# Small matmuls of four heads in one burst, RWKV's two heads in turn, and sixteen columns ahead of h

## The chip, the cores and the metric

The kernel runs on one core of a Trainium2 chip. The metric is device time in microseconds (us), lower is better. The profile names the engines PE (TensorE, matmuls), PEld (TensorE, weight loads), DVE (VectorE), ACT (ScalarE), POOL (GpSimd) and SP (SyncE, which here issues most DMAs).

## The reference

A trunk of two layers on one sequence of 1024 tokens with 1024 features, all in float32. Of each layer this matters here:

```python
h = _rmsnorm(x, norm1_g[l]) * (1.0 + sc1) + sh1
(rw_r, rw_k, rw_v, gl_q, gl_k, gl_v, gl_g,
 rt_q, rt_k, rt_v, rt_g) = jnp.split((h @ w_in[l]).astype(f32), splits, axis=-1)
...
y = jnp.concatenate([y_a, y_b, y_c], axis=-1).astype(x.dtype) @ w_out[l]
x = x + gt1 * y
h = _rmsnorm(x, norm2_g[l]) * (1.0 + sc2) + sh2
x = x + gt2 * ((jax.nn.silu(h @ ffn_w_gate[l]) * (h @ ffn_w_up[l])) @ ffn_w_down[l])
```

`y_a` is RWKV-7 time mixing with 8 heads of 64. `y_b` is gated linear attention (GLA) and `y_c` is retention, each with 4 heads, keys of 32 and values of 64, in chunks of 64 tokens: inside a chunk scores times values, and between chunks a carried state:

```python
att = jnp.sum(q_[:, :, :, None, :] * k_[:, :, None, :, :] * dec, axis=-1)
return jnp.einsum('bhnm,bhme->bhne', att, v_)
...
inter = jnp.einsum('nbhcd,nbhde->nbhce', qc * jnp.exp(bc), s_prev)
```

## The kernel before

**Layout and halves.** Activations lie transposed, features on the 128 partitions and tokens along the columns. The sequence is worked in two halves of 512 tokens, so x is 8 tiles of 128x512 for each half. The order is: projection of layer 0 half 0, then of half 1; output projection and FFN of half 0; output projection of half 1 and projection of layer 1 half 0; FFN of layer 0 half 1; and so on with layer 1, one half behind the other.

**Dense matmuls.** `dense` (L200 to L211) makes one 128x512 output tile. Weights and activations are split into a high and a low float32r part, so each of 8 k steps has three matmuls: high weight on high activation (L207), high weight on low activation (L208), low weight on high activation (L209). Two PSUM banks named `psd` take turns. The weight tile is cast on ACT (L186) and its low part is made on POOL (L187).

**h.** The normalised activations are 16 tiles `h` (8 k steps, high and low), made in `norm_h` (L290 to L319). Each is 514 columns wide: the 512 tokens start at the third column, and the second column holds the last token of the half before, so that the LoRA matmuls of RWKV can read h shifted by one token (`hact(h, 1)`, L327). The FFN's own intermediate, `gh` and `gl`, lies in tiles of 512 columns that are read from the first.

**Streams.** The small work of the heads is written as Python generators. A generator yields a cost; `pump` (called in `dense` after each k step with 0.65) gives each stream that much times its rate, and the stream goes on while it has credit. So instructions of the streams are placed between dense matmuls in program order, each behind the dense matmul it follows. The rates are 1.8 for the heads and mixers of layer 0 half 0, 1.5 for RWKV's preparations that run ahead of them, and 0.8 for the rest. Waiting is left to semaphores. All engines run their own instructions in order. The constants AT1 to AT5, GL1 to GL4 and PR1 to PR9 are the costs that are yielded; `drain` runs what is left.

**PSUM for the streams.** `pmx` (L592 to L595) hands out banks in the turn pm, yA, px, yB, pm, yu, where pm has two buffers: six banks. RWKV with two units at once (layer 0 half 0) takes px and yB in turn for the matmuls here.

**GLA and retention** (`Attn`, L628 to L712). `scores` (L653 to L662) loops over 4 heads; for each it takes a bank, makes 8 matmuls, one for each chunk (L660: 32 rows of keys, 64x64 out, into the upper or lower half of the partitions by the chunk's parity), hands the bank to a sink, and yields AT1. GLA (L717 to L757) calls it 7 times: once with plain q and k (the sink copies on ACT), and once at each of 6 levels of blocks with decayed q and k (the sink is a predicated copy on DVE, L745). Retention calls it once (L774). `finish` (L664 to L712) transposes the keys, makes the chunk states (L672 on PE, L683 on DVE), and then for each head makes 8 matmuls scores times values (L697, 64 rows) and 8 matmuls query times state (L699, 32 rows) into one bank, yields AT5, copies it out on ACT (L701), and after each two heads calls `norm_tok` (L606 to L625).

**RWKV** (`rwkv`, L783). Each half of a layer has 4 units. `prep` of a unit builds W and bk, then for two groups of 4 chunks and the two heads j (rows 0 to 63 and 64 to 127) makes 4 matmuls (L871, 64 rows, 128 columns of weights and 128 of output) into a bank, which DVE masks into GB and W (L875, L876); PR3 is yielded after each.

An fp32 matmul of the program shows in the profile as two MATMUL instructions.

Of the kernel before, what the change touches and what calls it, by code (L numbers as in the profile page):

```python
# [10 lines left out]
F32 = mybir.dt.float32  # L11
F32R = mybir.dt.float32r
# [29 lines left out]
XV = 2  # L42
PR1 = 4.0
PR2 = 3.0
PR3 = 0.8
PR4 = 0.5
PR5 = 1.0
PR6 = 3.2
# [3 lines left out]
CH1 = 1.0  # L52
CH2 = 1.0
CH3 = 1.5
AT1 = 0.8
AT2 = 1.0
AT3 = 0.7
AT4 = 0.25
AT5 = 1.0
GL1 = 1.0  # L60
GL2 = 2.0
GL3 = 1.5
GL4 = 1.0
# [2 lines left out]
WHB = 3  # L66
WLB = 3
XPB = 11
AHEAD = 60
RATEP = 1.5  # L70
RATEN = 1.0
# [23 lines left out]
def trunk_kernel(ctx, tc, xT, cT, ada_w, pv, wfm, wo, wg, wu, wd, l1w, l2a, l2g, l2c,  # L95
# [3 lines left out]
    V, A, G, T, SY = nc.vector, nc.scalar, nc.gpsimd, nc.tensor, nc.sync  # L99
# [31 lines left out]
    def f32(ap):  # L131
        return ap.bitcast(F32)
# [126 lines left out]
    def rstd_of(x, idle=None):  # L259


        acc = wp.tile([128, 512], F32, tag="nr", name="acc", bufs=1)
        if idle:
            ps = bank()
        for k in range(KT):
            if idle:
                sq = idle.tile([128, 512], F32, tag="sq", name="sq", bufs=5)
            else:
                sq = acc if k == 0 else wp.tile([128, 512], F32, tag="n", name="sq", bufs=2)
            A.activation(out=sq, in_=x[k], func=AF.Square)  # L270
            if idle:
                T.matmul(ps, om, sq, start=k == 0, stop=k == KT - 1)
                if k == 0:

                    A.activation(out=lnt, in_=sq[:, 0:1], func=AF.Ln, bias=eps)
            elif k:
                V.tensor_tensor(out=acc, in0=acc, in1=sq, op=ALU.add)  # L277
        yield 8.0
        if not idle:
            ps = bank()  # L280
            T.matmul(ps, om, acc, start=True, stop=True)
        A.activation(out=acc, in_=ps, func=AF.Ln, bias=eps)
        rstd_last[:] = [A.activation(out=acc, in_=acc, func=AF.Exp, scale=-0.5).ins]
        yield 1.0
        return acc

    rstd_last = []
    hlast = {}

    def norm_h(x, l, hf, which, h, pool=hp, r=None, mods=None, E=V, idle=None):  # L290

        if r is None:
            r = yield from rstd_of(x, idle)
        gs = par.tile([128, 8], F32, name="gs", tag=f"gs{which}")
        g = P(l, "n1g" if which == 0 else "n2g")
        if mods is None:
            V.scalar_tensor_tensor(out=gs, in0=mod[l][:, 3 * which + 1, :], scalar=1.0, in1=g, op0=ALU.add, op1=ALU.mult)
        if which == 0 and hf == 0:
            hlast[l] = par.tile([128, KT, 2], F32, name="hlast", tag="hlast")
        for k in range(KT):  # L300
            h.append([pool.tile([128, 514], F32R, tag="h", name="h", bufs=16) for _ in range(2)])
            sh = mod[l][:, 3 * which, k:k + 1]
            t = wp.tile([128, 512], F32, tag="n", name="nt", bufs=2)
            hi, lo = (h[k][j][:, 2:514] for j in range(2))
            if mods is not None:
                mods(k)
                V.scalar_tensor_tensor(out=gs[:, k:k + 1], in0=mod[l][:, 3 * which + 1, k:k + 1], scalar=1.0, in1=g[:, k:k + 1],
                                       op0=ALU.add, op1=ALU.mult)
            (V if k < XV else E).tensor_tensor(out=t, in0=x[k], in1=r, op=ALU.mult)
            A.activation(out=t, in_=t, func=AF.Identity, scale=gs[:, k:k + 1], bias=sh)  # L310
            split(t, hi, lo, E)
            if which == 0:
                for j in range(2):
                    if hf == 0:
                        G.memset(f32(h[k][j][:, 0:2]), 0.0)
                        G.tensor_copy(hlast[l][:, k, j:j + 1], f32(h[k][j][:, 513:514]))
                    else:
                        G.tensor_copy(h[k][j][:, 1:2], hlast[l][:, k, j:j + 1])
            yield 1.0  # L319

    def norm_now(*a, **kw):
# [3 lines left out]
        return h  # L325

    def hact(h, shift=0):  # L327
        return lambda k, part: h[k][part][:, 2 - shift:514 - shift]

    xs_d = [[dram.tile([128, 512], F32, name=f"xs{k}{j}") for j in range(2)] for k in range(KT)]  # L330
    y_d = [[None if k < 4 else dram.tile([128, 512], F32, name=f"y{k}{j}") for j in range(2)] for k in range(KT)]
# [255 lines left out]
    R2 = [slice(0, 64), slice(64, 128)]  # L587
# [4 lines left out]
    def pmx(of="all"):  # L592

        cyc[of] += 1
        return bank4(BANKS[of][cyc[of] % len(BANKS[of])])  # L595
# [32 lines left out]
    class Attn:  # L628
# [23 lines left out]

        def scores(self, kd, qd, sink):  # L653

            for h in range(4):
                r = slice(32 * h, 32 * h + 32)
                ps = pmx()
                for c in range(8):
                    cc = slice(c * 64, c * 64 + 64)
                    T.matmul(ps[R2[c % 2], (c // 2) * 64:(c // 2) * 64 + 64], kd[r, cc], qd[r, cc], start=True, stop=True)  # L660
                sink(h, ps[:, :256].rearrange("p (a n) -> p a n", a=4))
                yield AT1  # L662

        def finish(self, att, qd, kd, dec, centre, scale):  # L664
            pool, hf, key = self.pool, self.hf, "S" + self.g
# [19 lines left out]
                yield AT4  # L685
            if hf == 0:
                G.tensor_copy(carry[key], Sa[:, 8, :])
            Ys = []
            for hp_ in range(2):
                Y = self.t("gqe", 2).rearrange("p (a j e) -> p a j e", a=4, j=2)  # L690
                for j in range(2):
                    h = 2 * hp_ + j
                    r = slice(32 * h, 32 * h + 32)
                    o = pmx()
                    oc = [o[R2[c % 2], (c // 2) * 64:(c // 2) * 64 + 64] for c in range(8)]
                    for c in range(8):
                        T.matmul(oc[c], att[h][R2[c % 2], c // 2, :], self.v(h, c), start=c < 2, stop=False)  # L697
                    for c in range(8):
                        T.matmul(oc[c], qd[r, c * 64:c * 64 + 64], Sa[r, c, :], start=False, stop=c > 5)  # L699
                    yield AT5  # L700
                    A.copy(Y[:, :, j, :], o[:, :256].rearrange("p (a e) -> p a e", a=4))  # L701
                Ys.append(Y.rearrange("p a j e -> p (a j) e"))
                norm_tok(Ys[-1], pool, self.tmp, EPS, centre)
            yield FY
# [78 lines left out]
    def rwkv(l, hf, ip, pool, B=1):  # L783
# [33 lines left out]
        def prep(q, k1, r1, v1, wt, sa):  # L817
# [47 lines left out]

            GB = pool.tile([128, 8, 128], F32, tag="GB", name="GB", bufs=B)
            for a in (0, 4):
                for j, r in enumerate(R2):
                    o, ps = R2[1 - j], ppx()
                    for c in range(a, a + 4):  # L870
                        T.matmul(ps[:, (c - a) * 128:(c - a) * 128 + 128], bk[r, c].rearrange("p s t -> p (s t)"), W[r, c, j, :],  # L871
                                 start=True, stop=True)
                    p3 = ps.rearrange("p (a t) -> p a t", a=4)
                    mk = gmask.unsqueeze(1).to_broadcast([128, 4, 128])
                    V.tensor_tensor(out=GB[r, a:a + 4, :], in0=p3[r], in1=mk[r], op=ALU.mult)  # L875
                    V.tensor_tensor(out=W[o, a:a + 4, j, :], in0=p3[o], in1=mk[o], op=ALU.mult)  # L876
                    yield PR3
            gl = GB[:, :, 0:64]

            nd = dram.tile([32, 32, 32], F32, tag="nd", name="nd", bufs=3)  # L880
# [309 lines left out]
    with pool("x0") as x0:  # L1190
# [4 lines left out]
        h = []  # L1195
# [177 lines left out]
```

## Time and profile before

| | us |
|---|---|
| median of 3 runs | 3398.83 |
| lowest, highest | 3397.83, 3406.38 |
| the profiled execution | 3401.25 |
| its span, first to last instruction | 3399.5 |

The stages of the profiled execution, read from which lines evict the dense tiles: projection of layer 0 half 0 until about 345 us, of half 1 until 655, output projection and first FFN until 1390, projection of layer 1 half 0 until 1629, FFN until 2207, projection of layer 1 half 1 until 2445, output projections and FFN half 0 of layer 1 until 3030, and the last FFN half to the end. The heads of GLA and retention run beneath the projections, those of layer 0 half 1 beneath the output projection and the start of the first FFN. RWKV's units run beneath the FFNs, save those of layer 0 half 0, which run beneath the projection of half 1.

In the lines quoted below, a row of a stage view gives start and end, length, busy time of each engine with its count, the granted TensorE clock as a share of full speed, the DMA share and GB/s. A row of the timeline gives start, duration, engine, line, operation, output tile and inputs, shape and count, and in brackets the idle time before it with what ended it. Matmuls are pipelined: durations overlap, and the pace is read from start to start.

### The profile page before, as it was taken

What the parts mean: (1) busy time and instruction counts of PE and PEld (TensorE: products, weight loads), DVE (VectorE), ACT (ScalarE), POOL (GpSimd) and SP (SyncE); (2) the same over time, 40 slices, a digit from 0 to 9 for tenths busy, and PEclk for the clock granted to TensorE, in tenths of its full rate; (3) what the DMA queues carried; (4) which work ended last, traced back from release to release, by engine and by line L of the source; (5) the groups of instructions that cost most, each with busy time, mean ns of one, the idle gap of its engine ahead of it and who ended that gap; (6) DMA issues with size and microseconds to landing.
All of it is one profiled execution on the core that took longest, in us unless ns stands there. A gap on an engine that the chain in (4) does not pass through costs nothing. (4 is left out here: it accounts for less than half of the span.)

```text
span 3399.5 us, 47488 instructions
## 1 busy us (share of the span) xinstructions
PE 3049.9 (90%) x18162; PEld 2326.1 (68%) x18162; DVE 1994.5 (59%) x3747; ACT 1113.9 (33%) x1703; POOL 1234.7 (36%) x825
## 2 busy tenths in 40 slices
PE   6897888799888888999988999899997989999998
PEld 4664666476676676776766777677576767778886
DVE  6565777576776655536766663624666666452223
ACT  4324323243233223524322322542432322342222
POOL 6313333123334334532333434533232433444443
PEclk8988889799989898999988999999897989999999
DMA  6744535434544224434433322543533323332332
GB/s 230 239 157 142 169 110 156 153 103 128 147 129 113 88 84 133 156 90 146 129 98 86 87 70 87 161 130 112 155 83 88 105 80 94 120 109 87 105 92 82
DMA packets 266835, 411.01 MB, mean 121 GB/s; under 512 B 71152, under 2 KB 149424, under 8 KB 266608
## 3 DMA queue, kind: packets, MB, share of 16 engines
q1 hardware_dynamic: 211312, 393.28, 37.2%
q10 hardware_dynamic: 55296, 14.70, 2.1%
q8 instruction: 143, 2.34, 0.3%
q14 instruction: 84, 0.69, 0.1%
HBM read 343.92 MB, written 63.96 MB: 120 GB/s over the span
## 5 line engine op out<-in xcount | busy, mean ns | idle before, releaser
L187 POOL TENSOR_TENSOR wl<-wr,wh 128x1024 fp32r<-128x1024 f32 (+2 forms) x508 | 1028.6, 2027 | 1744.2 <-ACT wh L186 1653.2
L207 PE MATMUL psd<-h,wh 128*128 128x512 f32 (+1 forms) x2208 | 933.2, 423 | 112.7 <-DVE sg L1100 65.7
L208 PE MATMUL psd<-h,wh 128*128 128x512 f32 (+1 forms) x2208 | 908.1, 411 | 12.1 <-DVE h L195 12.0
L209 PE MATMUL psd<-h,wl 128*128 128x512 f32 (+1 forms) x2208 | 905.1, 410 | 0.0
L186 ACT CAST wh<-wr 128x1024 fp32r<-128x1024 f32 (+2 forms) x507 | 440.8, 871 | 1142.0 <-PE psd L208 582.2
L207 PEld LDWEIGHTS psd<-h,wh 128*128 128x128 f32 (+1 forms) x2208 | 432.1, 196 | 249.9 <-DVE sg L1100 74.3
L208 PEld LDWEIGHTS psd<-h,wh 128*128 128x128 f32 (+1 forms) x2208 | 434.7, 197 | 117.2 <-DVE h L195 15.8
L209 PEld LDWEIGHTS psd<-h,wl 128*128 128x128 f32 (+1 forms) x2208 | 433.7, 196 | 103.2 <-issue 2.4
L207 PE MATMUL psd<-gh,wh 128*128 128x512 f32 x960 | 401.0, 419 | 25.9 <-DVE x L1114 14.0
L208 PE MATMUL psd<-gl,wh 128*128 128x512 f32 x960 | 385.0, 401 | 6.1 <-DVE gl L195 6.1
L209 PE MATMUL psd<-gh,wl 128*128 128x512 f32 x960 | 384.0, 400 | 0.0
L207 PEld LDWEIGHTS psd<-gh,wh 128*128 128x128 f32 x960 | 184.7, 193 | 78.6 <-issue 24.1
L1114 DVE SCALAR_TENSOR_TENSOR x<-psd,mod,x 128x512 f32<-128x512 f32 x192 | 143.2, 748 | 130.0 <-PE psd L209 128.4
L208 PEld LDWEIGHTS psd<-gl,wh 128*128 128x128 f32 x960 | 185.6, 193 | 47.0 <-DVE gl L195 9.3
L209 PEld LDWEIGHTS psd<-gh,wl 128*128 128x128 f32 x960 | 185.4, 193 | 40.6 <-POOL wl L187 0.3
L914 DVE TENSOR_TENSOR tm<-X,nl 128x60 f32<-128x60 f32 (+24 forms) x496 | 189.0, 381 | 14.6 <-DMA nl<-nd 0.2
L242 DVE SCALAR_TENSOR_TENSOR aw<-aw,cb 128x1024 f32<-128x1024 f32 x96 | 128.4, 1341 | 100.0 <-DMA aw<-in_ada_w 75.8
L916 DVE TENSOR_TENSOR X<-X,tm 128x60 f32<-128x60 f32 (+24 forms) x496 | 165.1, 333 | 15.3
L1100 DVE SCALAR_TENSOR_TENSOR sg<-sg,psd 128x512 f32<-128x512 f32 x88 | 60.1, 683 | 194.1 <-ACT sg L1099 193.9
L1103 DVE SCALAR_TENSOR_TENSOR sg<-sg,psd 128x512 f32<-128x512 f32 x88 | 60.1, 683 | 141.0 <-PE psd L209 140.8
L195 DVE TENSOR_TENSOR gl<-sg,gh 128x512 fp32r<-128x512 f32 x88 | 96.3, 1094 | 37.0 <-ACT gh L194 36.9
L277 DVE TENSOR_TENSOR acc<-acc,sq 128x512 f32<-128x512 f32 x63 | 96.3, 1528 | 30.9 <-ACT sq L270 29.4
(459 smaller groups left out, 3526.6 us busy)
## 6 DMA issues: line engine op xcount, KB each, us to landing
aw<-in_ada_w SPq DMA_DIRECT2D x96, 512.0 KB, 3.9
wr<-in_wfm SPq DMA_DIRECT2D x96, 512.0 KB, 3.7
wr<-in_wg SPq DMA_DIRECT2D x88, 512.0 KB, 3.6
wr<-in_wu SPq DMA_DIRECT2D x88, 512.0 KB, 3.6
wr<-in_wd SPq DMA_DIRECT2D x128, 256.0 KB, 2.7
wr<-in_wo SPq DMA_DIRECT2D x32, 512.0 KB, 3.6
wr<-in_wd SPq DMA_DIRECT2D x64, 192.0 KB, 2.4
x<-in_xT SPq DMA_DIRECT2D x32, 256.0 KB, 4.5
```

Of the source, the lines that this page charges most:

```text
L186: (E.copy if E is A else E.tensor_copy)(wh[:, :n], wr[:, :n])
L187: WS.tensor_tensor(out=wl[:, :n], in0=wr[:, :n], in1=f32(wh[:, :n]), op=ALU.subtract)
L195: E.tensor_tensor(out=lo, in0=src, in1=f32(hi), op=ALU.subtract)
L207: T.matmul(ps[:M], sh, act(k, 0), start=(k == order[0]), stop=False)
L208: T.matmul(ps[:M], sh, act(k, 1), start=False, stop=False)
L209: mark[:] = [T.matmul(ps[:M], sl, act(k, 0), start=False, stop=(k == order[-1])).ins]
L242: V.scalar_tensor_tensor(out=w, in0=w, scalar=0.5, in1=cb, op0=ALU.mult, op1=ALU.mult, accum_out=mod[l][:, rnd, k:k + 1])
L277: V.tensor_tensor(out=acc, in0=acc, in1=sq, op=ALU.add)
L914: V.tensor_tensor(out=tm[:, :nr, :n], in0=X[:, :nr, s:s + 1].to_broadcast([128, nr, n]), in1=nl[:, s, s + 1:32].unsqueeze(1).to_broadcast( ...
L916: V.tensor_tensor(out=X[:, :nr, s + 1:32], in0=X[:, :nr, s + 1:32], in1=tm[:, :nr, :n], op=ALU.add)
L1100: V.scalar_tensor_tensor(out=sg, in0=sg, scalar=1.0, in1=pg, op0=ALU.add, op1=ALU.mult)
L1114: V.scalar_tensor_tensor(out=x[m], in0=ps, scalar=mod[l][:, 5, m:m + 1], in1=x[m], op0=ALU.mult, op1=ALU.add)
```

## The change

- The four heads' `scores` take four banks at once; the loop runs over chunks outside and heads inside; the four sinks follow, and AT1 is yielded once. In `finish` the output matmuls of all heads come first: scores times values by head, then query times state with chunks outside and heads inside; AT5 is yielded once; the copies and both `norm_tok` follow.
- In `prep` the two heads' matmuls take a bank each and alternate; the masking of both heads follows; PR3 is yielded once for the pair.
- Costs: PR3 0.8 to 1.6, AT1 0.8 to 1.2, AT5 1.0 to 1.5, GL1 1.0 to 3.0.
- Tiles of h get 16 columns ahead of the tokens instead of 2: 528 columns, data from the 17th, the last token of the half before in the 16th. The squares at the very start (L267) have 4 buffers instead of 5.

```diff
-PR3 = 0.8
+PR3 = 1.6
-AT1 = 0.8
+AT1 = 1.2
-AT5 = 1.0
-GL1 = 1.0
+AT5 = 1.5
+GL1 = 3.0
+HP = 16
...
-                sq = idle.tile([128, 512], F32, tag="sq", name="sq", bufs=5)
+                sq = idle.tile([128, 512], F32, tag="sq", name="sq", bufs=4)
...
-            h.append([pool.tile([128, 514], F32R, tag="h", name="h", bufs=16) for _ in range(2)])
+            h.append([pool.tile([128, HP + 512], F32R, tag="h", name="h", bufs=16) for _ in range(2)])
...
-            hi, lo = (h[k][j][:, 2:514] for j in range(2))
+            hi, lo = (h[k][j][:, HP:] for j in range(2))
...
-        return lambda k, part: h[k][part][:, 2 - shift:514 - shift]
+        return lambda k, part: h[k][part][:, HP - shift:HP + 512 - shift]
...
         def scores(self, kd, qd, sink):
+            ps = [pmx() for _ in range(4)]
+            for c in range(8):
+                cc = slice(c * 64, c * 64 + 64)
+                for h in range(4):
+                    r = slice(32 * h, 32 * h + 32)
+                    T.matmul(ps[h][R2[c % 2], (c // 2) * 64:(c // 2) * 64 + 64], kd[r, cc], qd[r, cc], start=True, stop=True)
             for h in range(4):
-                r = slice(32 * h, 32 * h + 32)
-                ps = pmx()
-                for c in range(8):
-                    cc = slice(c * 64, c * 64 + 64)
-                    T.matmul(ps[R2[c % 2], (c // 2) * 64:(c // 2) * 64 + 64], kd[r, cc], qd[r, cc], start=True, stop=True)
-                sink(h, ps[:, :256].rearrange("p (a n) -> p a n", a=4))
-                yield AT1
+                sink(h, ps[h][:, :256].rearrange("p (a n) -> p a n", a=4))
+            yield AT1
...
-            Ys = []
+            Ys, os_ = [], [pmx() for _ in range(4)]
+
+            def oc(h, c):
+                return os_[h][R2[c % 2], (c // 2) * 64:(c // 2) * 64 + 64]
+
+            for h in range(4):
+                for c in range(8):
+                    T.matmul(oc(h, c), att[h][R2[c % 2], c // 2, :], self.v(h, c), start=c < 2, stop=False)
+            for c in range(8):
+                for h in range(4):
+                    r = slice(32 * h, 32 * h + 32)
+                    T.matmul(oc(h, c), qd[r, c * 64:c * 64 + 64], Sa[r, c, :], start=False, stop=c > 5)
+            yield AT5
             for hp_ in range(2):
                 Y = self.t("gqe", 2).rearrange("p (a j e) -> p a j e", a=4, j=2)
                 for j in range(2):
-                    h = 2 * hp_ + j
-                    r = slice(32 * h, 32 * h + 32)
-                    o = pmx()
-                    oc = [o[R2[c % 2], (c // 2) * 64:(c // 2) * 64 + 64] for c in range(8)]
-                    for c in range(8):
-                        T.matmul(oc[c], att[h][R2[c % 2], c // 2, :], self.v(h, c), start=c < 2, stop=False)
-                    for c in range(8):
-                        T.matmul(oc[c], qd[r, c * 64:c * 64 + 64], Sa[r, c, :], start=False, stop=c > 5)
-                    yield AT5
-                    A.copy(Y[:, :, j, :], o[:, :256].rearrange("p (a e) -> p a e", a=4))
+                    A.copy(Y[:, :, j, :], os_[2 * hp_ + j][:, :256].rearrange("p (a e) -> p a e", a=4))
...
             for a in (0, 4):
+                pss_ = [ppx(), ppx()]
+                for c in range(a, a + 4):
+                    for j, r in enumerate(R2):
+                        T.matmul(pss_[j][:, (c - a) * 128:(c - a) * 128 + 128], bk[r, c].rearrange("p s t -> p (s t)"),
+                                 W[r, c, j, :], start=True, stop=True)
                 for j, r in enumerate(R2):
-                    o, ps = R2[1 - j], ppx()
-                    for c in range(a, a + 4):
-                        T.matmul(ps[:, (c - a) * 128:(c - a) * 128 + 128], bk[r, c].rearrange("p s t -> p (s t)"), W[r, c, j, :],
-                                 start=True, stop=True)
-                    p3 = ps.rearrange("p (a t) -> p a t", a=4)
+                    o, p3 = R2[1 - j], pss_[j].rearrange("p (a t) -> p a t", a=4)
...
-                    yield PR3
+                yield PR3
```

More of the change, by code (lines that the diff above doesn't have):

```diff
@@ L314, in norm_h @@
                     if hf == 0:
-                        G.memset(f32(h[k][j][:, 0:2]), 0.0)
-                        G.tensor_copy(hlast[l][:, k, j:j + 1], f32(h[k][j][:, 513:514]))
+                        G.memset(f32(h[k][j][:, HP - 2:HP]), 0.0)
+                        G.tensor_copy(hlast[l][:, k, j:j + 1], f32(h[k][j][:, HP + 511:HP + 512]))
                     else:
-                        G.tensor_copy(h[k][j][:, 1:2], hlast[l][:, k, j:j + 1])
+                        G.tensor_copy(h[k][j][:, HP - 1:HP], hlast[l][:, k, j:j + 1])
             yield 1.0
```

## The prediction

> **What bounds the kernel now.** I read the page first, then the busy time by stage, then TensorE's timeline around the edited lines.
>
> ```profile
> span 3399.5 us, 47488 instructions
> ```
> ```profile
> 0.00:830.00 830.00, 689.41 (x4813) 496.87 (x4814) 553.95 (x1130) 279.19 (x432) 265.94 (x202) 0.87 0.50 158
> 830.00:1390.00 560.00, 487.36 (x2708) 379.21 (x2707) 382.12 (x712) 176.01 (x276) 220.29 (x165) 0.91 0.40 120
> 1390.00:1629.00 239.00, 233.27 (x1673) 169.96 (x1672) 106.81 (x212) 92.94 (x142) 72.69 (x37) 0.95 0.42 136
> 1629.00:2207.00 578.00, 521.76 (x2882) 408.20 (x2881) 364.43 (x674) 184.73 (x290) 227.69 (x153) 0.92 0.34 98
> 2207.00:2445.00 238.00, 231.99 (x1668) 169.19 (x1667) 106.90 (x212) 90.14 (x131) 75.09 (x46) 0.95 0.44 136
> 2445.00:3030.00 585.00, 531.83 (x2898) 415.34 (x2897) 365.27 (x672) 188.83 (x292) 219.86 (x135) 0.92 0.33 94
> 3030.00:3399.50 369.50, 354.30 (x1531) 287.29 (x1529) 114.99 (x135) 102.07 (x144) 153.14 (x88) 0.99 0.32 96
> ```
> The columns after the length are busy time of PE, PEld, DVE, ACT and POOL, then the granted clock. PE is the busiest engine in every stage, but not equally. I group the stages by what runs behind the dense matmuls. **Q** (1390 to 1629, 2207 to 2445) is the projection of layer 1 with the GLA and retention heads behind it: PE is busy 465 of 477 us, 97.5%. **T** (from 3030) is the last FFN half alone, 96%. **F** is the three stretches of output projection and FFN with RWKV behind: 1541 of 1723 us, 89%. **I** is the first 830 us, 83%. So PE time that is removed should shorten Q and T almost one for one, F less, I least. My weights, chosen from those shares and from what fills the rest (waits for DVE), are 0.95, 1, 0.75 and 0.6.
>
> **Part A: h starts 64 bytes in, not 8.** At the end of the kernel both kinds of dense matmul run side by side, undisturbed (grouped lines, 3040 to 3380):
>
> ```profile
> L208 PE MATMUL psd<-h,wh 128*128 128x512 f32 x320 | 126.5, 395 | 0.0
> ...
> L208 PE MATMUL psd<-gl,wh 128*128 128x512 f32 x171 | 66.7, 390 | 0.0
> ```
> Same shape, same full clock, 5 ns apart. The visible difference is the moving operand: gl is read from its first column, h from its third. With the pad of 16, h starts at a round address as gl does, so I expect 390 ns. By the code each half of a layer has 1056 matmuls on h in its FFN and 648 in its projection (25 dense tiles of 24, and 48 of the LoRA; the other 48 read h shifted by one column and stay crooked). At 5 ns, times the granted clock, because at half clock the stream is far slower than any such step: I 1296 x 5 x 0.87 = 5.6 us, F 3168 x 5 x 0.92 = 14.5, Q 6.2, T 5.3; 31.6 in all. Bounds: 0 if the 5 ns has another cause, 37 if all of it comes back at any clock and the step is nearer 5.5. The writers of h (ACT, DVE, POOL) keep their shapes.
>
> **Part B: scores.** 32 calls (7 in each of 4 GLA runs, 1 in each retention) of 4 heads; a head is 8 matmuls, which the profile shows as 16. A single head between dense matmuls, in Q:
>
> ```profile
> 1520.21 0.40 PE L208 MATMUL psd<-h,wh 128*128 128x512 f32 x1
> 1520.44 0.40 PE L209 MATMUL psd<-h,wl 128*128 128x512 f32 x1
> 1520.77 0.68 PE L660 MATMUL yu<-gqe 32*64 32x64 f32 x16
> 1521.38 0.50 PE L207 MATMUL psd<-h,wh 128*128 128x512 f32 x1
> 1521.71 0.40 PE L208 MATMUL psd<-h,wh 128*128 128x512 f32 x1
> ```
> From 1520.44 to 1521.71 are 1.27 us, where two dense steps without the head take 2 x 0.23 (1520.21 to 1520.44 is one). A head costs PE 0.80 us, of which 0.1 on entering and 0.1 on leaving. Heads stand alone like this wherever the busy time of a stage is 32 x 0.68:
>
> ```profile
> 0.00:345.00 345.00, 15.85 (x512) 0.89 0.58 192
> 1390.00:1629.00 239.00, 21.77 (x512) 0.95 0.42 136
> ```
> In Q they do (32 x 0.68 = 21.8); I take the second half of layer 0 as the same. In the first half of layer 0 the stream runs faster and four heads already follow each other:
>
> ```profile
> 177.43 0.51 PE L660 MATMUL yB<-gqe 32*64 32x64 f32 x10
> ...
> 178.92 0.50 PE L208 MATMUL psd<-h,wh 128*128 128x512 f32 x1
> ```
> 177.43 to 178.92 is 1.5 us, with 0.1 for entering and 0.1 for leaving 1.7 us for 64. In the new order eight neighbours differ in rows (head) or output half (chunk). The trace has one group with eight different places, the state products of finish, 32 instructions:
>
> ```profile
> 1582.23 0.39 PE L209 MATMUL psd<-h,wl 128*128 128x512 f32 x1
> 1582.56 0.26 PE L672 MATMUL yA<-gvt,gkt 64*32 64x64 f32 x4
> ...
> 1582.78 0.24 PE L672 MATMUL px<-gvt,gkt 64*32 64x64 f32 x4
> 1582.94 0.50 PE L207 MATMUL psd<-h,wh 128*128 128x512 f32 x1
> ```
> The first 28 start within 0.22 us, under 8 ns each, and the group costs PE 0.71 - 0.23 + 0.1 = 0.58 (1582.23 to 1582.94, less a step, plus the leaving). With 32 more at 7.5 ns a burst of 64 is 0.82 us. So a call of four lone heads saves 4 x 0.80 - 0.82 = 2.4, one already in a row 1.7 - 0.82 = 0.9. Q: 16 x 2.4 = 38. I: 8 x 2.4 + 8 x 0.9 = 26. Sum 64; lower bound, if a burst can't beat the 1.7: 24 x 1.5 = 36. The sinks are the same instructions; they start after all four heads, and the next call takes two of its six banks from the call before, whose sinks stand ahead of the next level's exponentials on DVE, so the operands come last, not the banks. GL1 rises from 1 to 3 and a level's cost stays 4.2 (1 + 4 x 0.8; 3 + 1.2), so pace is unchanged and operands get more time.
>
> **Part C: outputs**, 8 calls of 4 heads.
>
> ```profile
> 1590.41 0.39 PE L209 MATMUL psd<-h,wl 128*128 128x512 f32 x1
> 1590.73 0.68 PE L697 MATMUL pm<-gvt,gatt 64*64 64x64 f32 x16
> 1591.34 0.68 PE L699 MATMUL pm<-Sa,gqd 32*64 32x64 f32 x16
> 1591.95 0.50 PE L207 MATMUL psd<-h,wh 128*128 128x512 f32 x1
> ```
> Now 1.54 - 0.23 + 0.1 = 1.41 a head, 5.6 a call. After: L697 keeps its order within a head (up to 4 x 0.61 = 2.4), L699 becomes a burst (0.6), 0.2 for the ends: 3.1. Saves 2.5 a call, 10 us in Q, 10 in I. What it costs: the four copies and both norm_tok now follow without a pause. Each norm_tok has four wide DVE passes at about this price, and thirteen small ones on 8 columns:
>
> ```profile
> 1606.21 0.69 DVE L612 TENSOR_TENSOR gqe<-gqe,mn 128x512 f32<-128x512 f32 x1
> 1606.81 0.68 DVE L625 TENSOR_TENSOR gqe<-gqe,rs 128x512 f32<-128x512 f32 x1
> ```
> 4 x 0.69 = 2.8, and with the small ones I estimate 5 us each, 10 together, queued ahead of the eviction of a dense tile, which lasts 24 x 0.23 = 5.5. Two PSUM banks cover one tile, so an eviction may be 4 us late: 0 to 4 us x 8. I take 0.5 x 8 = 4, since the small steps depend on each other and leave holes in which evictions fit.
>
> **Part D: RWKV's pair.** 16 units, each 4 groups of 4 matmuls, shown as 8.
>
> ```profile
> 0.00:3399.50 3399.50, 99.13 (x512) 0.92 0.40 121
> ```
> ```profile
> 1850.12 1.13 PE L871 MATMUL yA<-W,bk 64*128 64x128 f32 x8 [1.47 <-DVE bk L857]
> 1851.17 0.50 PE L207 MATMUL psd<-h,wh 128*128 128x512 f32 x1
> 1855.63 2.04 PE L871 MATMUL px<-W,bk 64*128 64x128 f32 x8 [3.96 <-DVE bk L858]
> ```
> A group is 1.13 us busy at full clock, 2.04 at half; 64 groups making 99.13 puts 45% at half. Whether heads in different row halves overlap when each fills all 128 columns is seen where two groups happened to meet:
>
> ```profile
> 324.80 0.27 PE L871 MATMUL px<-W,bk 64*128 64x128 f32 x1
> 324.80 0.27 PE L871 MATMUL yB<-W,bk 64*128 64x128 f32 x1
> 324.91 0.27 PE L871 MATMUL px<-W,bk 64*128 64x128 f32 x1
> ```
> They do, two per 0.11 us. So a pair lasts as long as one group did and one group per pair goes: 1.05 + 0.2 for the switch, 1.25 at full clock; about 2.3 at half, of which I count half, because the dense work that moves up runs at half clock too. 0.55 x 1.25 + 0.45 x 1.15 = 1.2, times 32 is 39. The first pair of a unit now waits for the second head's bk as well. In the rows above, what ran between 1850.12 and the wait of 3.96 (1.55 us) would move behind it, so there the pair gains nothing. I count first pairs at half: 29 in all, 22 in F and 7 in I. Bounds: 10 and 45. In the four units of layer 0's first half, which have two banks, the second pair also waits for four evictions: 4 x 0.5 = 2 us.
>
> **Rest.** sq with 4 buffers instead of 5:
>
> ```profile
> 6.73 10.04 PE L272 MATMUL psd<-sq,om 128*128 128x512 f32 x16 [6.73 <-ACT sq L270]
> ```
> eight matmuls at 1.25 us are the chain there, and a square need be only one ahead: nothing; without that cover it would be one square. AT1 and AT5 make a run of heads cheaper in the planner: 2 for GLA's scores, 2 for retention's, 2.5 for each finish, 9 in all. They end earlier beneath the projection, and their fetches of the gates and stores of y on SP's queue move with them in the same order; I take 2 us for each Q, between nothing and the 9 units' own length of some 12.
>
> **Sum.** Q (6.2 + 38 + 10) x 0.95 = 51; T 5; F (14.5 + 22) x 0.75 = 27; I (5.6 + 26 + 10 + 7) x 0.6 = 29; 112, less 6 for new waits, plus 4: **110 us**. The profiled execution took 3401.25, 2.4 over the median shown. 3401.25 - 110 - 2.4 = **3289 us**.
>
> **Rivals.** *Bursts no faster than now.* The rows of L672 speak against it: its instructions start under 8 ns apart; for it, that its weights are 32 columns wide and L660's 64. B falls to 24 and 11 in Q and I from 38 and 26, and L699 costs 1 more a call: 16 x 0.95 + 15 x 0.6 + 6 = 30 lost, 3319. The Trainium skill, TensorE: Matmul & The Clock Gate, "Wait — 56ns, not 53.3ns?", says much the same: start to start never drops below about 25 ns however small the matmul. By that rule a burst of 64 is an estimated 1.6 us; the trace's L672 disagrees with it.
>
> *h's 5 ns isn't the start address.* Nothing else differs in the rows, but h and gl also lie in different pools. Without A: 5.9 + 5.3 + 10.9 + 3.4 = 25 less, 3314.
>
> *Only Q and T gain*: in F and I what PE saves it waits longer for DVE, which is busy two thirds of the time there. 56 - 6 = 50, 3349. Against: PE is at 89% in F.
>
> *Fewer stalls, less throttling.* 8% of the clock is lost, 272 us' worth; a sixth less is 45 us more gain, 3244.
>
> *Slower: the first pair of each unit stalls PE so long that it drops to half clock.* The 3.96 us wait above is followed by a group at 2.04. If each of 16 units pays 1.5 us and then 8 us more because some 8 us of PE work runs at half clock, that is 152 against 110: 3441. It decides from 7 us per unit. Against: these windows already exist at that place. The same page of the Trainium skill (Part 1, The HAM clock gate) gives an idle window of about 3.4 us for the drop to half, and the trace agrees: 2.04 behind 3.96.
>
> *No change*: the compiler's order undoes the bursts, and A gives nothing; no row speaks for it.
>
> **Chances.** Forecast 0.60, bursts no faster 0.08, h 0.07, only Q and T 0.12, throttling 0.06, no change 0.03, slower 0.04. A difference of 0.3%, 10 us, is about what a measurement of this kernel can tell. Faster 0.93, same 0.03, slower 0.04. The range takes in the bounds of A, B and D around the sum and reaches to 3349 and near 3244: 3238 to 3350.
>
> **What would show it.** Dense matmuls on h at 390 ns in the last stage. L660 in bursts of 64 within about 0.65 us, busy time of its stages near 8 x 0.85 instead of 21.8. L871 of both heads alternating, 16 within 1.1 us. Q shorter by some 25 us each, F by 9 each, T by 5. Wrong, if Q keeps its length, if idle time in front of L871 grows past 100 us, or if the clock of F falls below 0.90.

## The result and the profile after

| | before | after |
|---|---|---|
| median, us | 3398.33 | 3278.89 |
| lowest, highest | 3382.08, 3406.38 (4 runs) | 3277.06, 3285.87 (4 runs) |
| the profiled execution's span | 3399.5 | 3278.2 |

The ratio is 0.9655, 95% interval 0.9634 to 0.9676: 119 us faster. The forecast was 3289, with 3238 to 3350 as its range. The stages of the kernel after, cut at the same dense matmuls as before (columns as in the prediction's stage view):

```profile
span 3278.2 us, 47479 instructions
```
```profile
0.00:810.00 810.00, 646.11 (x4822) 468.58 (x4823) 567.75 (x1146) 281.54 (x437) 269.21 (x205) 0.88 0.52 166
810.00:1348.00 538.00, 479.34 (x2700) 373.41 (x2699) 378.29 (x697) 172.71 (x272) 214.82 (x162) 0.93 0.40 120
1348.00:1570.00 222.00, 210.46 (x1674) 157.33 (x1673) 110.80 (x212) 93.70 (x143) 72.66 (x38) 0.94 0.46 147
1570.00:2129.00 559.00, 504.23 (x2880) 394.20 (x2879) 362.82 (x674) 183.82 (x289) 228.52 (x153) 0.95 0.35 101
2129.00:2345.00 216.00, 204.76 (x1669) 153.52 (x1668) 112.88 (x212) 89.89 (x131) 75.69 (x47) 0.96 0.46 148
2345.00:2910.00 565.00, 513.68 (x2900) 403.46 (x2899) 365.12 (x672) 189.09 (x293) 221.03 (x135) 0.95 0.34 98
2910.00:3278.20 368.20, 352.92 (x1528) 286.48 (x1526) 115.07 (x135) 101.54 (x143) 153.02 (x88) 0.98 0.31 96
```

| stage | predicted gain | measured gain | PE busy time less |
|---|---|---|---|
| I, to 810 | 29 | 20 | 43 |
| F, three stretches | 27 | 61 | 44 |
| Q, two stretches | 51 | 39 | 50 |
| T, the end | 5 | 1 | 1 |
| sum, without the prediction's -6 and +4 | 112 | 121 | 138 |

The sum came out, the distribution didn't. F gave twice its forecast, and more than its PE time fell; its granted clock rose from between 0.91 and 0.92 to between 0.93 and 0.95. I, Q and T gave less.

The parts, as the trace after shows them. Line numbers have moved: dense L208 to L210, scores L662, outputs L698 and L702, RWKV's pair L877. **Scores**, one burst in Q on the timeline:

```profile
1430.01 0.39 PE L484 MATMUL psd<-h,wl 128*128 128x512 f32 x1
1430.32 0.27 PE L662 MATMUL yB<-gqe 32*64 32x64 f32 x1
1430.33 0.27 PE L662 MATMUL pm<-gqe 32*64 32x64 f32 x1
...
1431.02 0.22 PE L662 MATMUL pm<-gqe 32*64 32x64 f32 x1
1431.17 0.50 PE L482 MATMUL psd<-h,wh 128*128 128x512 f32 x1
1431.50 0.39 PE L483 MATMUL psd<-h,wh 128*128 128x512 f32 x1
```
All 64 start within 0.70 us, 11 ns apart in the mean. The burst costs PE 1.16 (1430.01 to 1431.17) - 0.23 + 0.1 = 1.03 us, against four heads at 0.80 before. The busy time of L662 over the stage says the same (21.77 us before in Q, 15.85 at the start):

```profile
0.00:339.00 339.00, 8.01 (x512) 0.89 0.60 197
1348.00:1570.00 222.00, 7.30 (x512) 0.94 0.46 147
```

**Outputs**, one call in Q:

```profile
1518.35 0.40 PE L210 MATMUL psd<-h,wl 128*128 128x512 f32 x1
1518.68 0.68 PE L698 MATMUL yB<-gvt,gatt 64*64 64x64 f32 x16
...
1520.13 0.63 PE L698 MATMUL pm<-gvt,gatt 64*64 64x64 f32 x16
1520.69 0.27 PE L702 MATMUL yB<-Sa,gqd 32*64 32x64 f32 x1
...
1521.38 0.22 PE L702 MATMUL pm<-Sa,gqd 32*64 32x64 f32 x1
1521.53 0.50 PE L208 MATMUL psd<-h,wh 128*128 128x512 f32 x1
```
3.18 - 0.23 + 0.1 = 3.05 us a call. The 64 of L702 start within 0.69 us, where head by head they took about 0.6 us for each head.

**RWKV's pair**, one unit (the brackets are PE's idle time before the row and what ended it):

```profile
1784.85 1.13 PE L877 MATMUL yA<-W,bk 64*128 64x128 f32 x8 [1.48 <-DVE bk L863]
1785.91 0.50 PE L208 MATMUL psd<-h,wh 128*128 128x512 f32 x1
...
1790.36 2.04 PE L877 MATMUL px<-W,bk 64*128 64x128 f32 x8 [3.95 <-DVE bk L864]
...
1793.48 0.58 PE L877 MATMUL yB<-W,bk 64*128 64x128 f32 x1
1793.49 0.58 PE L877 MATMUL pm<-W,bk 64*128 64x128 f32 x1
...
1795.14 0.42 PE L877 MATMUL pm<-W,bk 64*128 64x128 f32 x1
1795.49 0.79 PE L208 MATMUL psd<-h,wh 128*128 128x512 f32 x1
```
The first pair still runs head by head with dense matmuls between, as in the program before: the compiled order puts each head where its operands are ready, so there is no joint wait. The second pair alternates, 16 instructions in 2.01 us, where one head alone took 2.00 at half clock (1862.33 to 1864.33 below). Over the whole kernel that is rarer than one unit suggests: both heads take turns from end to end in the second pair of five of the 16 units, all in F, and in none of the four units before 600 us.

**h**, in the last stage (2920 to 3258, grouped lines):

```profile
L209 PE MATMUL psd<-h,wh 128*128 128x512 f32 x320 | 125.7, 393 | 0.0
L209 PE MATMUL psd<-gl,wh 128*128 128x512 f32 x171 | 66.6, 389 | 0.0
```
The gap of 5 ns has become 4. From start to start, the mean over these matmuls went from 232.9 ns to 231.2 on h, against some 227 on gh and gl.

### The profile page after: what moved, and what is told of

Read it like the earlier page. It is cut to its first block, busy times and chain, and to the rows that moved or that the text cites. A ratio compares the mean times of both kernels' runs of the same rounds, so it can differ in the third digit from the quotient of the medians.

```text
span 3278.2 us, 47479 instructions
## 1 busy us (share of the span) xinstructions
PE 2911.5 (89%) x18162; PEld 2237.0 (68%) x18162; DVE 2012.7 (61%) x3747; ACT 1112.3 (34%) x1703; POOL 1235.0 (38%) x825
## 5 line engine op out<-in xcount | busy, mean ns | idle before, releaser
L208 PE MATMUL psd<-h,wh 128*128 128x512 f32 (+1 forms) x2208 | 918.1, 416 | 91.1 <-DVE sg L1107 38.7
L209 PE MATMUL psd<-h,wh 128*128 128x512 f32 (+1 forms) x2208 | 896.0, 406 | 8.5 <-DVE h L196 8.5
L210 PE MATMUL psd<-h,wl 128*128 128x512 f32 (+1 forms) x2208 | 895.8, 406 | 0.0
L208 PEld LDWEIGHTS psd<-h,wh 128*128 128x128 f32 (+1 forms) x2208 | 426.7, 193 | 222.2 <-DVE sg L1107 45.7
L209 PEld LDWEIGHTS psd<-h,wh 128*128 128x128 f32 (+1 forms) x2208 | 428.1, 194 | 113.7 <-DVE h L196 11.2
L210 PEld LDWEIGHTS psd<-h,wl 128*128 128x128 f32 (+1 forms) x2208 | 427.1, 193 | 99.8 <-issue 1.9
L208 PE MATMUL psd<-gh,wh 128*128 128x512 f32 x960 | 395.2, 413 | 37.8 <-DVE X L923 12.4
L210 PE MATMUL psd<-gh,wl 128*128 128x512 f32 x960 | 382.3, 398 | 0.0
L208 PEld LDWEIGHTS psd<-gh,wh 128*128 128x128 f32 x960 | 184.3, 192 | 92.4 <-issue 31.1
L210 PEld LDWEIGHTS psd<-gh,wl 128*128 128x128 f32 x960 | 184.6, 192 | 40.7 <-POOL wl L188 0.8
L921 DVE TENSOR_TENSOR tm<-X,nl 128x60 f32<-128x60 f32 (+24 forms) x496 | 192.4, 388 | 15.2 <-DMA nl<-nd 0.6
L243 DVE SCALAR_TENSOR_TENSOR aw<-aw,cb 128x1024 f32<-128x1024 f32 x96 | 137.9, 1440 | 94.3 <-DMA aw<-in_ada_w 80.8
L923 DVE TENSOR_TENSOR X<-X,tm 128x60 f32<-128x60 f32 (+24 forms) x496 | 150.0, 302 | 15.2
L278 DVE TENSOR_TENSOR acc<-acc,sq 128x512 f32<-128x512 f32 x63 | 85.2, 1352 | 27.0 <-ACT sq L271 25.3
```

The lines of the kernel that those rows point to most:

```text
L208: T.matmul(ps[:M], sh, act(k, 0), start=(k == order[0]), stop=False)
L209: T.matmul(ps[:M], sh, act(k, 1), start=False, stop=False)
L210: mark[:] = [T.matmul(ps[:M], sl, act(k, 0), start=False, stop=(k == order[-1])).ins]
L243: V.scalar_tensor_tensor(out=w, in0=w, scalar=0.5, in1=cb, op0=ALU.mult, op1=ALU.mult, accum_out=mod[l][:, rnd, k:k + 1])
L921: V.tensor_tensor(out=tm[:, :nr, :n], in0=X[:, :nr, s:s + 1].to_broadcast([128, nr, n]), in1=nl[:, s, s + 1:32].unsqueeze(1).to_broadcast( ...
L923: V.tensor_tensor(out=X[:, :nr, s + 1:32], in0=X[:, :nr, s + 1:32], in1=tm[:, :nr, :n], op=ALU.add)
```

## Experiments

Two theories stood first. Mine: the gain comes from the parts with the prices above, F's surplus through the clock. The rival: the parts matter little by themselves, and the new costs or the wandering of half-clock windows make the gain. Medians are of the kernel and of the kernel before on the same chip.

### One part alone, four kernels

```diff
+HP = 16
...
-            hi, lo = (h[k][j][:, 2:514] for j in range(2))
+            hi, lo = (h[k][j][:, HP:] for j in range(2))
```
Above: the columns ahead of h alone, with the tile, its edges and `sq` as in the change. The second kernel has the change's `scores`, AT1 and GL1 alone; the third its `finish` and AT5; the fourth its `prep` and PR3.

> The kernel before with the 16 columns ahead of h alone (and 4 buffers for the squares). Theory, from the changed kernel's last stage, where h's matmuls went from 395 to 394 ns and that stage by 1.3 us: 1.6 ns start to start on 6816 matmuls, 8 to 11 us less, about 3389. Rival, the prediction's step A (5 ns, 25 us less after weighting): 3373. Rival, nothing: 3398.

> The kernel before with the scores in one burst alone, with AT1 1.2 and GL1 3.0. Theory: a burst costs PE about 1.0 us where four lone heads cost 3.2, 24 calls x 2.2 and a little from the first stage: 45 to 55 us less, about 3348. Rival, the saving sits in the planner's cheaper costs and in the clock, not in the burst: under 25 us less, over 3373.

> The kernel before with the output matmuls first and together, AT5 1.5. Theory: 2.5 us of PE in each of 8 calls, 14 to 20 us less, about 3382. Rival, the two normalisations in a row on DVE hold up evictions and give it back: 3395 or more.

> The kernel before with RWKV's two heads in turn alone, PR3 1.6. Theory: the first pair of a unit runs one head behind the other as before, because the second head's bk is later; 16 to 20 pairs of 32 save one group of 1.25 to 2.3 us: 20 to 28 us less, about 3374. Rival, all the waiting stays and what PE saves it waits longer for DVE: within 8 us of 3398.

| alone | median | before | ratio, 95% | gain |
|---|---|---|---|---|
| h's columns | 3395.21 | 3401.77 | 0.9985, 0.9971 to 0.9998 | 7 |
| scores | 3318.26 | 3401.77 | 0.9770, 0.9747 to 0.9793 | 84 |
| outputs | 3372.95 | 3401.77 | 0.9921, 0.9901 to 0.9942 | 29 |
| pair | 3356.06 | 3401.77 | 0.9868, 0.9844 to 0.9892 | 46 |

They add up to some 165, where all together gave 119 on this measure, so the gains don't add. Three of the four gained more than was expected of them: scores 84 for 45 to 55, outputs 29 for 14 to 20, the pair 46 for 20 to 28. Much of the surplus lies in F, where neither scores nor outputs run. Scores alone took 37 us off F in its profiled execution, of 71 in all. Outputs alone took 36 off F, of 38 in all, and the first FFN lasted 540 us, not 560.

```profile
833.40:1373.50 540.10, 480.94 (x2703) 372.95 (x2702) 379.32 (x699) 175.37 (x275) 214.90 (x163) 0.94 0.42 123
```
That is the stage of the kernel with outputs alone. PE is busy 6 us less there than before, idle 13 less, and its clock is 0.94 instead of 0.91. The four RWKV units beneath it begin 18 to 30 dense matmuls earlier than before; in the two later FFN stretches they begin at the same ones. In Q outputs alone gave 3.0 and 2.5 us, scores alone 15.2 and 14.5, together 18.2 and 17.0 where the change has 17.3 and 22.0: in Q the parts add, within some 5 us. No kernel takes the scores out of the change.

### One part taken out of the change, two kernels

```diff
-PR3 = 1.6
+PR3 = 0.8
-                pss_ = [ppx(), ppx()]
-                for c in range(a, a + 4):
-                    for j, r in enumerate(R2):
...
                 for j, r in enumerate(R2):
+                    o, ps = R2[1 - j], ppx()
+                    for c in range(a, a + 4):
...
-                yield PR3
+                    yield PR3
```
Above: the pair as before, all else as in the change. The other has `finish` and AT5 as before.

> The changed kernel without RWKV's pair (the heads as before, PR3 0.8). Theory: the pair's gain sits at each unit's own place, 4 to 7 us with a shorter half-clock stretch, and is kept beside the others: 30 to 45 us slower than the changed kernel, 3310 to 3324. Rival, the parts share one gain (alone they make 155 us, together 119): 10 to 20 us slower.

> The changed kernel without the output burst (AT5 1.0 a head as before). Theory: alone it gained 20 us of its 27 in the first FFN, where nothing of it runs, only because RWKV started elsewhere against the dense tiles; the scores do that too, so here it is worth what it saves in its own stages: 3 to 10 us slower, 3282 to 3289. Rival, it adds up as alone: 27 us slower, 3306.

Without the pair: 3337.19 (3330.53 to 3348.35), ratio to before 0.9815 (0.9788 to 0.9842). So in the change the pair is worth 58 us, or 54 when each is set against the kernel before on its own chip: more than alone, and more than the 30 to 45 that I expected. Without the output burst: 3279.14 (3269.64 to 3289.77), ratio 0.9647 (0.9620 to 0.9675), the same as the change. In the change, the burst of outputs is worth nothing that can be measured. What outputs alone had gained in the first FFN, this kernel has without them:

```profile
809.80:1336.80 527.00, 471.38 (x2704) 367.19 (x2704) 371.33 (x699) 174.64 (x275) 214.07 (x162) 0.94 0.43 126
```

### The order of the small matmuls alone

```diff
-            for c in range(8):
-                cc = slice(c * 64, c * 64 + 64)
-                for h in range(4):
-                    r = slice(32 * h, 32 * h + 32)
+            for h in range(4):
+                r = slice(32 * h, 32 * h + 32)
+                for c in range(8):
+                    cc = slice(c * 64, c * 64 + 64)
...
-                for c in range(a, a + 4):
-                    for j, r in enumerate(R2):
+                for j, r in enumerate(R2):
+                    for c in range(a, a + 4):
```
The change with its bursts, banks and costs, but head by head in each: neighbours share their rows and can't overlap across row groups.

> The changed kernel with the same bursts, banks and costs, but heads outside and chunks inside in the scores and in query times state, and RWKV's two heads one behind the other: nothing overlaps between heads except at their seams. Theory: the overlap of row groups is worth 0.65 us in each of 32 score bursts (21 us), 1.3 us in each of 8 output bursts (10) and all of the pair's 45 us measured alone, less what they share: 40 to 70 us slower than the changed kernel, 3320 to 3350. Rival, the bursts gain because PE switches less often between dense and small matmuls, and because of the costs: within 15 us of 3279.

3315.76 (3307.33 to 3320.51) against 3399.70, ratio 0.9753 (0.9730 to 0.9776). Of the gain, 37 us hang on the alternating order, a little under the 40 to 70 expected; they hold the overlap between row groups and what it does to the clock (below). The other 84 remain with heads in a row. Fewer switches between dense and small matmuls, sinks that follow together and the other parts can make them; they were not told apart. The rival that the order within a burst carries little falls by the 37; so does a reading that it carries nearly all. By stage it loses most in the second FFN stretch, 18.5 us, where of the three parts only the pair runs.

### The costs alone

```diff
-AT1 = 1.2
+AT1 = 3.2
...
-AT5 = 1.5
-GL1 = 3.0
+AT5 = 4.0
+GL1 = 1.0
```


> The changed kernel with the old totals of the costs: AT1 3.2, AT5 4.0, GL1 1.0, so that heads end as late as before and a level's matmuls follow its exponentials as closely as before. Theory: matmuls count, costs little: 5 to 15 us slower, from waits for the decayed q and k and from heads that end beneath the LoRA's last part. Rival, the new costs carry a good part: over 25 us slower.

3286.70 (3278.32 to 3294.56), ratio 0.9674 (0.9652 to 0.9696): 8 us above the change. The pace that the costs set carries little of the gain.

### Where h starts, four kernels

```diff
+        hpad = 0 if pool is not hp else HP
-            h.append([pool.tile([128, HP + 512], F32R, tag="h", name="h", bufs=16) for _ in range(2)])
+            h.append([pool.tile([128, hpad + 512], F32R, tag="h", name="h", bufs=16) for _ in range(2)])
...
```
The first: in the last FFN half alone, h has tiles of 512 columns, as gh and gl have.

> The changed kernel, where h of the last FFN half alone lies in tiles of 512 columns (2048 bytes apart, as gh), read from the first. Theory, from the pattern over k in that stage (matmuls on h repeat every 12 before, every 6 after, as the addresses of h modulo 256 bytes do, while gh, with one residue, is even at 227): 231 to 227 ns start to start, 1056 x 4 = 4 us off the last stage. Rival, h is slower than gh for what runs beside it (gate and up against down): the stage keeps 231 and its length.

```diff
-XPB = 11
-HP = 16
+XPB = 10
+HP = 64
...
-                sq = idle.tile([128, 512], F32, tag="sq", name="sq", bufs=4)
+                sq = idle.tile([128, 512], F32, tag="sq", name="sq", bufs=3)
```
The second: 64 columns ahead everywhere, with one buffer less for x and for the squares to make room.

> The changed kernel with 64 columns ahead of h instead of 16, so that all h tiles lie 2304 bytes apart and start at gh's residue modulo 256 bytes; to make room, x has 10 buffers instead of 11 and the squares at the start 3 instead of 4. Theory: 4 ns less on 6816 matmuls, 15 to 25 us faster than the changed kernel, near 3260. Rival, the start address does nothing more: 3279, or a few us slower for the buffers.

```diff
-HP = 64
+HP = 56
...
-            h.append([pool.tile([128, HP + 512], F32R, tag="h", name="h", bufs=16) for _ in range(2)])
+            h.append([pool.tile([128, 576], F32R, tag="h", name="h", bufs=16) for _ in range(2)])
...
-            hi, lo = (h[k][j][:, HP:] for j in range(2))
+            hi, lo = (h[k][j][:, HP:HP + 512] for j in range(2))
```
The third and fourth: the same tiles of 576 columns, with the tokens from column 56 (above) or 48.

> As with 64 columns ahead (tiles 2304 bytes apart), but h starts at column 56: one start address for all, a whole multiple of 256 bytes, where the weights start 32 past one. Theory that the start must match the weights': over 228 ns start to start on h in the last stage (229 to 235, like the mixed starts). Rival, that round starts are what counts: 227 or less.

> The same with column 48: all h start 224 past a multiple of 256, 64 bytes behind the weights' residue. Theory that the start must match the weights': 229 to 235 ns on h. Rival, that any one start for all tiles, on a multiple of 32 bytes, will do: 227.

What I compare is the address modulo 256 bytes, the remainder after whole blocks of 256. Tiles lie one behind the other, so the length of a tile sets how their starts step: 528 columns are 8 x 256 + 64 bytes, 576 are 9 x 256, and 512 are 8 x 256; 514 are 8 x 256 + 8, which the built programs round up, so that these step by 32. The steps show in the traces: the pace of the matmuls on h in the last stage repeats every 12 of them before and every 6 in the change. Where the steps start from is read off the built programs and stands in no trace: there the weights wh and wl, and gh and gl, all start at 32.

| kernel | h starts, modulo 256 bytes | ns, start to start on h | T, us, against the change |
|---|---|---|---|
| before | all multiples of 32, plus 8 | 232.9 | +0.6 |
| the change | 32, 96, 160, 224 | 231.2 | 0 |
| 512 columns, last half | 32 | 226.8 | -4.3 |
| 64 columns ahead | 32 | 226.8 | -5.3 |
| tokens from column 56 | 0 | 233.4 | +1.1 |
| tokens from column 48 | 224 | 233.4 | +2.0 |

The last column is the stage from the same dense matmul on; single executions. The mean durations show the same, here for 512 columns, then 64 ahead, then column 56 (grouped lines of the last stage):

```profile
L209 PE MATMUL psd<-h,wh 128*128 128x512 f32 x318 | 123.7, 389 | 0.0
L209 PE MATMUL psd<-gl,wh 128*128 128x512 f32 x152 | 59.1, 389 | 0.0
```
```profile
L209 PE MATMUL psd<-h,wh 128*128 128x512 f32 x299 | 116.3, 389 | 0.0
```
```profile
L209 PE MATMUL psd<-h,wh 128*128 128x512 f32 x323 | 127.7, 396 | 0.0
L209 PE MATMUL psd<-gl,wh 128*128 128x512 f32 x152 | 59.2, 389 | 0.0
```
Between the second of these and the third only the offset in the tile differs, by 32 bytes. Even the roundest address, 0, is slow. h reaches gl's pace where all its tiles start as the weights and gl do. In the change, where by the table one tile in four starts there, none of the six places of the pattern has it: they take 229, 230, 231, 233, 232 and 232 ns. Whether h must match the weights or must be at 32 itself is not separated, since the weights never moved.

As times: 512 columns in the last half 3280.11 (ratio 0.9655, 0.9634 to 0.9676), its few us lost in the scatter; 64 columns everywhere **3259.83** (3259.46 to 3261.26), ratio 0.9595 (0.9576 to 0.9614). That version beats both kernels, the change by 19 us. Column 56 and column 48, one run each, 3285.83 and 3288.02: room and buffers are the same, so the 26 and 28 us to column 64 (some 3 less when each is set against the kernel before on its own chip) are put down to the start, within the scatter of one run.

## Why the prediction was right, and where not

**Sum.** 110 forecast, 119 measured. PE time removed: 145 forecast, 138 in the busy column. Prices from rows around one instance, times a count, held for B and C to 0.2 us a call. That the sums lie so near is in part luck all the same: A's PE time is an estimated 21 us short (1.7 ns where 5 were counted, of 31.6) and B's some 6, and what D brought beyond its 29 made up for them. In the sum of the rival *bursts no faster* there is a slip: 38 to 24 is 14, not 16, so 28 would be lost, 3317.

**A, the step that failed.** "With the pad of 16, h starts at a round address as gl does, so I expect 390 ns". The cause was right, as the kernels with 56 and 64 columns ahead show: start addresses set the 5 ns. The rule was wrong. A round start within the tile isn't a round start in memory: tiles of 528 columns step by 64 bytes modulo 256. The step is 1.7 ns (232.9 to 231.2), not 5; alone A gives 5 to 7 us, not 25. With every start at 32 the kernel gains 19 more, so about the 25 were there to be had. The rival that the 5 ns isn't the start address was right on A's small price and wrong on its reason. T gave 1 us of 5 for this.

**B.** A burst was forecast at 0.82 us and costs 1.03. The group of L672 from which I extrapolated starts 28 instructions at 8 ns; 64 come to 11. So a call saves 2.2 instead of 2.4 us. The rival that bursts are no faster, 1.7 us, is refuted. So is, for neighbours in different row groups, the figure beside it: the Trainium skill, TensorE: Matmul & The Clock Gate, "Wait — 56ns, not 53.3ns?", has no start to start below about 25 ns, where the trace has 64 within 0.70 us. Q still fell short of its forecast: PE is idle 23 us in Q, 12 before, so some of what PE saved went into waits.

**C.** The price held, 3.05 us a call against 3.1, but taking it out costs nothing that can be measured. In the profiled executions the first Q is as long without it and the second 8 us longer, together a little under the price of 10, and F, where none of it runs, is 17 us shorter, with 174 us at half clock against 194. That execution is at the low end of its kernel's runs (3269.64, median 3279.14), so part of the 17 is scatter; whether F's share returns with every such edit stays open.

**D, mis-sized.** Forecast 29 in PE, some 21 at the end; measured 46 alone and 54 to 58 within the change. First, "the first pair of a unit now waits for the second head's bk as well" is wrong: the compiled order runs it head by head in 14 of the 16 units. That also disposes of the rival on the slower side, a stall of each first pair: in the unit shown the waits on L863 and L864 are still 1.48 and 3.95, and over the kernel PE sits idle 48 us for bk in front of these matmuls, 51 before. Second, and more, "of which I count half, because the dense work that moves up runs at half clock too": the alternating pair doesn't only save time at half clock, it ends the half clock sooner. The same unit, cut at the same dense matmuls, first before, then after, without the pair, and with the order head by head (whole-stage columns, granted clock third from the end):

```profile
1840.20:1882.00 41.80, 36.36 (x146) 28.14 (x145) 29.70 (x43) 11.73 (x20) 18.00 (x7) 0.80 0.45 130
```
```profile
1774.90:1811.90 37.00, 31.56 (x146) 24.68 (x145) 29.23 (x42) 11.80 (x20) 17.64 (x7) 0.86 0.52 145
```
```profile
1801.80:1843.20 41.40, 35.97 (x146) 27.91 (x145) 29.03 (x42) 11.77 (x20) 17.88 (x7) 0.79 0.46 131
```
```profile
1791.80:1831.00 39.20, 33.78 (x147) 26.52 (x147) 29.42 (x43) 11.84 (x20) 17.58 (x7) 0.83 0.50 139
```
The pair is worth 4.4 us here (41.4 without it in the change, 37.0 with it), and before to after is 4.8. In the trace's clock record the half-clock time of this unit is 17.07, 10.24, 17.07 and 13.65 us. 6.83 us less at half clock are an estimated 3.4 us of PE work sooner; the rest of the 4.8, 1.4, is about the group that went. Before, the clock stays at half although PE is busy without a gap from 1855.63 on, until the groups of L871 are past:

```profile
1862.33 2.07 PE L871 MATMUL pm<-W,bk 64*128 64x128 f32 x8
1864.33 0.79 PE L207 MATMUL psd<-h,wh 128*128 128x512 f32 x1
...
1869.19 0.75 PE L891 MATMUL pm<-cs_t,bk 128*128 128x128 f32 x4
1869.69 0.48 PE L207 MATMUL psd<-h,wh 128*128 128x512 f32 x1
```
After, the pair ends at 1795.49 and the dense step at 1796.81 runs at full clock. Summed over the record:

| half-clock time, us | whole span | F's three stretches |
|---|---|---|
| before | 545 | 96, 89, 92 |
| h's columns alone | 563 | 113, 99, 85 |
| scores alone | 494 | 82, 72, 82 |
| outputs alone | 501 | 68, 72, 85 |
| change without the pair | 524 | 85, 85, 75 |
| change, head by head | 495 | 72, 96, 68 |
| pair alone | 457 | 89, 51, 68 |
| the change | 456 | 75, 58, 61 |
| change without output burst | 433 | 58, 55, 61 |
| change, old costs | 460 | 87, 48, 68 |

The second and third stretches tell what the alternation does, since of the streams that were changed RWKV's alone runs beside their dense matmuls. Taken together they have 154 to 184 us at half clock and last 1143 to 1163 us in the six kernels that make one head's matmuls after the other's (the first six rows). In the eight that have the alternating pair (the last four rows and the four kernels of other starts) it is 109 to 136 us, and they last 1118 to 1130. The kernel with head by head order has the pair's place and cost and yet lies with the first group (164 us, 1149), so it is the alternation that counts there: 29 us between the means, where the whole of D was to bring 21. Its two stretches, to be read against the change's rows further up (559 and 565 us, 504.23 and 513.68 busy, clock 0.95 in both):

```profile
1576.80:2154.70 577.90, 521.86 (x2881) 408.27 (x2880) 362.53 (x674) 184.24 (x290) 227.73 (x153) 0.92 0.34 99
2378.50:2949.30 570.80, 518.84 (x2898) 407.13 (x2897) 365.46 (x672) 188.64 (x292) 220.45 (x135) 0.94 0.34 96
```
The first stretch doesn't sort itself this way: 68 to 113 us at half clock without the alternation, 58 to 89 with it. What the pair gives there and in I isn't separated from where RWKV's units happen to begin.

F has 83 us less at half clock, and PE was busy in 70 of them, 238 of 277 before and 168 of 194 after. Half of that is an estimated 35 us of the 61. In the first FFN edits of the outputs alone moved the half-clock time from 96 to 68 and from 75 to 58, in opposite senses of the edit; that is where outputs alone found 20 of the 38 us of their profiled execution, and it may be why the change can do without them. "Fewer stalls, less throttling" stood as a rival at 0.06, with a sixth less: half-clock time did fall by a sixth, 545 to 456. It belonged in the forecast as a term of D; that the total stayed near the forecast all the same is the luck named above.

**Weights.** One for one in Q was too much (0.78, 39 of 50), 0.75 in F too little (61 of 44). "Only Q and T gain" is refuted by F. **Costs and sq** at nothing to 4: 8 us for the costs, nearly as small as thought.

## What to carry to other kernels

Where TensorE drops to half clock, look at what runs while it should recover: here small matmuls on half or a quarter of the rows, one head after another, went with windows that stayed at half, and alternating row groups with windows that rose, which in the unit shown was worth more (an estimated 3.4 of 4.8 us) than the group of matmuls saved. Where one kind of matmul streams slower than another of the same shape, compare their start addresses modulo 256 bytes, and choose a tile's length, not only the offset in it, so that every tile starts as the fast ones do. Gains that a part shows alone are not its worth in the whole; take it out again before keeping its complexity.

## What the runs showed of the hardware that was not expected

**What ends a half-clock window.** The clock record knows only 1.0 and 0.5. Half-clock time comes in multiples of 3.41 us, but for the last stretch, which runs past the end of the kernel; this agrees with the window of 3413 ns in the Trainium skill, TensorE: Matmul & The Clock Gate, Part 1: The HAM clock gate. That page has the clock rise after one busy window; in these traces busy is not enough.

I cut the record of all fourteen traces into windows of 3.41 us and took those at half clock in which PE was over 90% occupied. I sorted them by the share of the window that went to matmuls on 32 or 64 rows alone, with no neighbour into another bank starting within 30 ns:

| share on part of the rows alone | clock rose after | of windows |
|---|---|---|
| under 0.1 | 603 | 610 |
| 0.1 to 0.2 | 56 | 70 |
| 0.2 to 0.3 | 62 | 123 |
| 0.3 to 0.4 | 20 | 105 |
| 0.4 to 0.5 | 5 | 72 |
| over 0.5 | 2 | 210 |

Where RWKV's pair takes turns for over half of the window, the clock rose after all 30, although these too use 64 rows at a time. The sorting was made on seven of the traces; the other seven gave the same picture (312 of 315 in the first row, 2 of 78 in the last, 22 of 22 for the pairs). The share of full rows and alternating groups can also be taken over all windows: from half clock it rose in 658 of 670 above 0.85 and in 4 of 665 below 0.5; from full clock it fell in 699 of 810 below 0.4 and in 7 of 10287 above 0.55. So in these traces it takes more to rise than to stay. The sorting is read off the traces and no kernel was made to test its limits, but the kernels with and without the alternation in F, above, moved as it says.

**The start address.** 226.8 ns for a 128x512 matmul whose moving operand starts at 32 modulo 256 bytes, 233.4 at 0 or 224, 3% apart, with the weights at 32 throughout; the addresses are those of the built programs.
